# Two-layer hybrid backbone on one core: the order of the token blocks after the attention of the first layer

## The chip, the core and the metric

The kernel runs on one core of a Trainium2 chip, with its own engines: TensorE (PE: matmuls and transposes; PEld is its weight load), VectorE (DVE), ScalarE (ACT), GpSimd (POOL), and SyncE (SP), which issues the transfers. The metric is the device time of one execution in microseconds (us); less is better. A difference of 0.2% is 6.3 us.

## The reference

Two layers act on 1024 latent tokens and 256 context tokens, 1024 features each, in float32:

```python
def hybrid_layer(x, xc, c_act, cctx_act, ...):
    sh1, sc1, g1, sh2, sc2, g2 = split(c_act @ w_mod + b_mod, 6)     # and the same for the context
    u  = modulate(rmsnorm(x, n1), sh1, sc1) @ w_in                   # uc from xc
    ym = mlstm(u...); yn = neighbourhood_attention(u...); yl = rg_lru(u...)
    x = x + g1 * (concat([ym, yn, yl]) @ w_out)
    x = x + g2 * (square(relu(modulate(rmsnorm(x, n2), sh2, sc2) @ w1)) @ w2)
    # the context too, in the first layer alone
```

The modulation vectors of a layer (`c_act @ w_mod`, 6144 columns) depend on the conditioning only, so those of layer 1 can be computed anywhere in layer 0.

## The kernel before, in words

The residual stream is kept feature-major: 1024 features are 8 tiles of 128 partitions (K tiles), tokens lie along the free axis. The tokens form three blocks: block 0 is the context (256), blocks 1 and 2 are the halves of the latents (512 each). A matmul of 128x512 or 128x256 thus handles one K tile, one tile of 128 output columns and one block. Every float32 operand is split into a high and a low part (`xh`, `xlo`; `wh`, `wl`), and three matmuls make one product. ScalarE rounds the high part (L200 for weights, L210 for activations), VectorE subtracts for the low one (L201, L211).

The stages of a layer are the input projections with the mLSTM and the RG-LRU, the neighbourhood attention, the output projection, norm2 and the MLP. In the first layer:

- Attention. Half 0 of the output projection (the four K tiles that do not need the attention) is run between attention steps by `fill()`. A step of the attention ends with the transposes L688 and the products L714 and L718.
- Half 1 of the output projection. `y_load` (L1306) loads rows of the mixers' output `yT_d` into `yl` and splits them, K tile by K tile and, in a K tile, for blocks 0, 1, 2. The last K tile comes from the attention output `yr`. The buffer `yl` has three copies. `x_rows` (L1420) loads the residual `res`, L1325 are the matmuls, L1426 adds to the residual.
- `stat_add` (L373, L376, L377) squares each finished K tile on ScalarE and sums on GpSimd in `acc`; `stat_of` turns these sums over the partitions with TensorE (L383) and reduces them on VectorE (L385).
- `norm_block` takes the reciprocal root with small VectorE instructions (root steps, L167 to L180), spreads it with TensorE (L398), and then makes one K tile after the other: product (L410), `xh` (L411, ScalarE), `xlo` (L412).
- MLP. Eight groups of 512 hidden columns; each has four `w_mlp1` weights (projections L436) and four `w_mlp2` weights (matmuls L1477, added to the residual by L1481).

The work goes by `parts`, the sets of blocks that share a pass over the weights: `parts = [[0, 1], [2]]` (L1292) in layer 0, [[1], [2]] in layer 1. The first part goes through half 1 and norm2, then the second part through half 1; the first part goes through all MLP groups with the second's norm2 in group 0 (`ng`); then the second part's MLP, in the first groups of which the next layer's norm1 of the first part's blocks runs. The norm1 of the second part's blocks comes after the last group.

The modulation of layer 1 is 48 steps of `mod_step_e`: each loads 0.5 MB of `w_mod` (`mr`, L301) into a single buffer and makes, for two vectors, a product (L310) and seven products with sums (L312) on VectorE. `tick()` issues the next step; an MLP group calls it 8 times. Every two steps, TensorE transposes the products (L323) for the sum.

Program order is only a starting point: a scheduler orders the instructions of each engine ahead of time, and each engine then runs its queue in order; a waiting instruction holds back all that is behind it on its engine. Transfers issued by SyncE pass one hardware queue (q1). `issue_after` adds an edge to that order. PSUM banks are named by pools ("a", "b", "c", "p", "q"; tiles psa, psb, ...).

Of the kernel before, what the change touches and what calls it, by code (L numbers as in the profile page):

```python
# [21 lines left out]
P = 128  # L22
# [11 lines left out]
# column offsets inside the combined input projection  # L34
# [4 lines left out]
# token blocks: (offset, size, is_context)  # L39
# [3 lines left out]
def host_consts():  # L43
    """Arrays that depend on shapes alone."""
# [19 lines left out]
    # column mask: partitions (h, ic'), [3 column types, 32 key columns]  # L64
# [8 lines left out]
    # row mask: partitions (i', ic'), [group slot (1, 0), 12 key rows]  # L73
# [18 lines left out]
def backbone_kernel(ctx: ExitStack, tc: tile.TileContext, I, out, dbg=None):  # L92
# [9 lines left out]
    # the normalised blocks lie on one side, all else on the other; they change sides after each attention  # L102
# [23 lines left out]
    def bank(tag):  # L126
        """A PSUM bank; several tags take turns."""
# [37 lines left out]
    def rsqrt(x, tmp_i, tmp_z, y):  # L165
        """y = 1/sqrt(x) for positive x, to float32 accuracy (integer seed and Newton steps)."""
# [7 lines left out]
    def rsqrt_mean(ss, n, inv, tag):  # L174
        """1/sqrt(ss * inv + EPS) of a [P, n] tile of sums."""
# [10 lines left out]
    def load_w(src, shape, early=False):  # L186
        """Loads a float32 weight tile and splits it exactly into two float32r parts; early: in two steps, so that
        the first products start sooner."""
# [16 lines left out]
    def w_fm(w, l, c0, r0=0, kt=KT, cols=P):  # L205
        """Weight tile [P, kt, cols] of rows r0.. and columns c0.. of layer l."""
        return load_w(w[l, r0:r0 + kt * P, c0:c0 + cols].rearrange("(k p) c -> p k c", p=P), (kt, cols))
# [40 lines left out]
    # c_act, cctx_act: 32 columns per k tile (two used)  # L248
# [12 lines left out]
    def mod_step(l, j, rawpool, bufs, ptag, i=None):  # L261
        """128 modulation columns of both vectors; every fourth step finishes 512: of step j and the three before,
        or, when i says the place, of two steps each of shift and scale."""
# [32 lines left out]
    lastpe = [None]  # L296

    def mod_step_e(l, j, rawpool, bufs):
        """128 modulation columns without the column tiles: products and K tiles summed elementwise."""
        raw = rawpool.tile([P, KT, P], F32, name=nm("mr"), tag="mr", bufs=bufs)  # L300
        d = sp.dma_start(raw, I["w_mod"][l, :, j * P:(j + 1) * P].rearrange("(k p) c -> p k c", p=P))  # L301
        # the context needs only the first two vectors of the last layer
# [15 lines left out]
    def mod_sum(l, j, ns):  # L318
        """Sums over the partitions of the products of ns steps."""
# [262 lines left out]
    for l in range(DEPTH):  # L582
# [827 lines left out]
        with tc.tile_pool(name=f"mlp_{l}", bufs=1, reuse_waits="tile") as rp:  # L1410
# [109 lines left out]
            if not last:  # L1520
                run(next_norm(2))
# [35 lines left out]
```

## Time and profile before

| what | us |
|---|---|
| three runs | 3122.56, 3128.67, 3129.33 |
| median of the runs | 3128.67 |
| profiled execution, its span | 3122.6 |
| TensorE busy in the span | 3016.5 |

The profiled span equals the lowest of the runs to the last digit shown, so the execution has nothing measurable around its span. The busy time of TensorE can hide a low clock: the windows give the granted clock beside it, 1.00 being the full one. A wait is shown at the instruction that waits; its releaser is the instruction that came last.

### The profile page before, as it was taken

How to read it: one execution, taken by the hardware profiler on the slowest of the kernel's cores; microseconds unless marked ns; L12 is line 12 of the kernel's file. 1: busy time of each engine (PE TensorE's matmuls, PEld its weight loads, DVE VectorE, ACT ScalarE, POOL GpSimd, SP SyncE). 2: the span in 40 equal slices, each digit the busy share in tenths (PEclk: the TensorE clock that was granted, in tenths of full speed). 3: DMA queues.
4: the chain of work that ended last, by engine and by line, in shares of the span. 5: the costliest groups of instructions: out<-in, count | busy, mean ns of one | idle time of the engine just before them, and what ended most of it. 6: DMA issues, size and time to landing. Idle time of an engine off the chain costs nothing.

```text
span 3122.6 us, 47473 instructions
## 1 busy us (share of the span) xinstructions
PE 3016.5 (97%) x18250; PEld 2553.0 (82%) x18250; DVE 1898.7 (61%) x4318; ACT 1129.1 (36%) x2011; POOL 288.9 (9%) x252
## 2 busy tenths in 40 slices
PE   7999998999899999999999999998899999999999
PEld 6888887878788888887778889997787777887877
DVE  5757654887887666455444584755787444444444
ACT  4632223674422222233222453234564223332222
POOL 0410010122200000010000511002222000000000
PEclk9999999999899999999999999999999999999999
DMA  9624667865233444233333532348753332343333
GB/s 272 223 73 124 174 172 206 234 186 176 67 109 109 123 127 124 79 108 99 92 94 95 176 122 82 101 123 222 223 169 113 95 95 88 99 117 90 93 96 93
DMA packets 531098, 410.73 MB, mean 132 GB/s; under 512 B 27580, under 2 KB 496536, under 8 KB 530872
## 3 DMA queue, kind: packets, MB, share of 16 engines
q1 hardware_dynamic: 519448, 387.41, 42.1%
q0 software_dynamic: 8576, 15.00, 1.5%
q10 hardware_dynamic: 2848, 5.28, 0.6%
q8 instruction: 144, 2.36, 0.3%
q14 instruction: 82, 0.67, 0.1%
HBM read 339.72 MB, written 67.53 MB: 130 GB/s over the span
## 4 chain that ended last, share of the span: by engine, by line
PE 70%; DVE 11%; DMA 10%; issue 2%; ACT 2%; SPq 1%; POOL 0%; ACTq 0%; DVEq 0%; POOLq 0%
PE psa L436 15%; PE psa L1477 14%; PE psq L436 5%; PE psp L436 5%; PE psp L1477 5%; PE psq L1477 5%; PE psp L451 4%; DMA mr<-in_w_mod_dram 4%; PE psq L451 4%; PE psp L1325 2%; DVE ma L312 2%; PE psc L718 2%; DVE wl L201 1%; PE psa L1325 1%; PE psb L688 1%
## 5 line engine op out<-in xcount | busy, mean ns | idle before, releaser
L200 ACT ACTIVATE wh<-wr 128x1024 fp32r<-128x1024 f32 (+3 forms) x356 | 361.6, 1021 | 946.5 <-PE psa L1477 307.3
L201 DVE TENSOR_TENSOR wl<-wr,wh 128x1024 fp32r<-128x1024 f32 (+3 forms) x356 | 425.0, 1198 | 386.4 <-ACT wh L200 380.0
L436 PE MATMUL psa<-xlo,wh 128*128 128x512 f32 (+1 forms) x856 | 319.7, 374 | 2.2 <-DVE xlo L412 2.2
L436 PE MATMUL psa<-xh,wh 128*128 128x512 f32 (+1 forms) x856 | 319.4, 373 | 2.4 <-ACT xh L411 2.3
L436 PE MATMUL psa<-xh,wl 128*128 128x512 f32 (+1 forms) x856 | 319.6, 373 | 1.4 <-DVE wl L201 1.4
L1477 PE MATMUL psa<-hl,wh 128*128 128x512 f32 (+1 forms) x768 | 286.0, 373 | 0.6 <-DVE hl L211 0.6
L1477 PE MATMUL psa<-hh,wh 128*128 128x512 f32 (+1 forms) x768 | 284.2, 375 | 0.3 <-ACT wh L200 0.3
L1477 PE MATMUL psa<-hh,wl 128*128 128x512 f32 (+1 forms) x768 | 277.9, 373 | 0.6 <-DVE wl L201 0.6
L1481 DVE SCALAR_TENSOR_TENSOR res<-psa,modt,res 128x512 f32<-128x512 f32 (+1 forms) x192 | 131.0, 693 | 170.3 <-PE psa L1477 169.9
L436 PEld LDWEIGHTS psa<-xh,wh 128*128 128x128 f32 x856 | 162.1, 190 | 33.4 <-ACT xh L411 3.1
L436 PEld LDWEIGHTS psa<-xlo,wh 128*128 128x128 f32 x856 | 162.1, 189 | 33.1 <-DVE xlo L412 2.6
L436 PEld LDWEIGHTS psa<-xh,wl 128*128 128x128 f32 x856 | 162.1, 189 | 32.3 <-DVE wl L201 2.2
L377 POOL TENSOR_TENSOR acc<-acc,nsq 128x512 f32<-128x512 f32 (+1 forms) x56 | 77.9, 1401 | 1026.9 <-ACT nsq L376 976.5
L1477 PEld LDWEIGHTS psa<-hh,wh 128*128 128x128 f32 x768 | 144.3, 188 | 34.6 <-ACT wh L200 8.6
L451 PE MATMUL psp<-wl,xh 128*128 128x256 f32 (+1 forms) x560 | 164.0, 293 | 4.3 <-DVE wl L201 4.2
L1477 PEld LDWEIGHTS psa<-hh,wl 128*128 128x128 f32 x768 | 144.3, 188 | 28.7 <-DVE wl L201 1.5
L1477 PEld LDWEIGHTS psa<-hl,wh 128*128 128x128 f32 x768 | 144.4, 188 | 27.4 <-DVE hl L211 0.8
L210 ACT ACTIVATE hh<-rl 128x512 fp32r<-128x512 f32 (+1 forms) x160 | 93.5, 589 | 202.1 <-DVE rl L1453 202.0
L451 PE MATMUL psp<-wh,xh 128*128 128x256 f32 (+1 forms) x560 | 161.9, 289 | 2.4 <-ACT wh L200 2.4
L451 PE MATMUL psq<-wh,xh 128*128 128x256 f32 (+1 forms) x560 | 161.7, 289 | 1.4 <-ACT usq L605 0.9
L451 PE MATMUL psq<-wl,xh 128*128 128x256 f32 (+1 forms) x560 | 160.6, 287 | 0.0
L451 PE MATMUL psp<-wh,xlo 128*128 128x256 f32 (+1 forms) x560 | 159.9, 286 | 0.0
(409 smaller groups left out, 7328.5 us busy)
## 6 DMA issues: line engine op xcount, KB each, us to landing
wr<-in_w_mlp_dram SPq DMA_DIRECT2D x256, 512.0 KB
mr<-in_w_mod_dram SPq DMA_DIRECT2D x92, 512.0 KB
wr<-in_w_in_dram SPq DMA_DIRECT2D x48, 512.0 KB
tab<-T_d SPq DMA_DIRECT2D x48, 384.0 KB
T_d<-E_d POOLq DMA_DIRECT2D x48, 256.0 KB, 6.6
ab<-row_d SPq DMA_DIRECT2D x36, 256.0 KB
xT_d<-res SPq DMA_DIRECT2D x4, 2048.0 KB
wr<-in_w_out_dram SPq DMA_DIRECT2D x32, 256.0 KB
```

Of the source, the lines that this page charges most:

```text
L200: act.activation(hi[:, a:b], raw[:, a:b], AF.Copy)
L201: dve.tensor_sub(lo[:, a:b], raw[:, a:b], hi[:, a:b].bitcast(F32))
L210: act.activation(hi, src32, AF.Copy)
L312: dve.scalar_tensor_tensor(a, raw[:, k], s[:, k], a, op0=OP.mult, op1=OP.add)
L377: pool.tensor_add(acc[bi], acc[bi], sq[:, :n])
L436: m = pe.matmul(t[:, :n], w[a][:, k, :], X[bi][b][:, k, :], start=(i == 0), stop=(i == 23))
L451: pe.matmul(t[:, :cols], X[bi][b][:, half * 4 + k, o:o + P], ws[half][a][:, k, :], start=(i == 0), stop=(i == 23))
L688: pe.transpose(t[:w, j * P:(j + 1) * P], S[e][:, o:o + w], permT)
L718: pe.matmul(to[64 * e:64 * e + 64, :P], vals[i][:w, 64 * e:64 * e + 64], PT[:w, e, i], start=(i == 0), stop=(i == nt - 1))
L1325: pe.matmul(t[:, :n], w[a][:, k, cc * P:(cc + 1) * P], Y[bi][b][:, k], start=(i == 0), stop=(i == 11))
L1477: m = pe.matmul(t[:, :n], w[a][:, k, cc * P:(cc + 1) * P], H[bi, k][b], start=(i == 0), stop=(i == 3 * GH - 1))
L1481: dve.scalar_tensor_tensor(xr[bi][:, ct], t[:, :n], G2[:, ct, v:v + 1], xr[bi][:, ct], op0=OP.mult, op1=OP.add)
```

## The change

There are five edits. (1) In layer 0 the parts become [[2], [0, 1]]: block 2 goes first through the fill, half 1, norm2 and the MLP, then blocks 0 and 1 together. `norms2` runs the norm2 of blocks 0 and 1 one after the other within the first part's MLP groups. The norm1 of layer 1 runs within the second part's MLP for block 2, and after it for blocks 0 and 1; the LRU projections of layer 1 begin with block 2 (XR and GT are the recurrence's input and gate columns). `y_load` keeps its order over the blocks. (2) Where a norm has `acc` (both norm2 and norm1 of layer 1), the root steps hold their operands `x` and `z` in the PSUM bank `rb` into which the root is spread later. (3) `tick()` stands after the `w_mlp1` weights alone, so four a group. (4) The remaining steps come at the end of the second part (`tick(64)`). (5) The VectorE instructions of the first modulation step are ordered behind the last `xlo` of block 2's norm2 (`lastlo`, `held`). The rest of the change removes comments.

```diff
     def norm_block(l, which, bi, xt, ss, tp, res, acc=None):
...
-        rs = rsqrt_mean(ss, nt, 1.0 / D, f"nr{nt}")
         rb = bank("b")
+        if acc:
+            ti = sm.tile([P, nt], I32, name=nm("ri"), tag=f"nr{nt}i")
+            rs = sm.tile([P, nt], F32, name=nm("ry"), tag=f"nr{nt}y")
+            x, z = rb[:, 0:nt], rb[:, 8:8 + nt]
+            dve.tensor_scalar(x, ss, 1.0 / D, EPS, op0=OP.mult, op1=OP.add)
+            dve.tensor_scalar(ti, x.bitcast(I32), 1, None, op0=OP.arith_shift_right)
+            dve.tensor_scalar(rs.bitcast(I32), ti, -1.0, float(0x5F3759DF), op0=OP.mult, op1=OP.add)
+            for _ in range(3):
+                dve.scalar_tensor_tensor(z, rs, -0.5, x, op0=OP.mult, op1=OP.mult)
+                dve.tensor_mul(z, z, rs)
+                dve.scalar_tensor_tensor(rs, z, 1.5, rs, op0=OP.add, op1=OP.mult)
+        else:
+            rs = rsqrt_mean(ss, nt, 1.0 / D, f"nr{nt}")
...
-            dve.scalar_tensor_tensor(lo[:, k], t, SH[:, k, v:v + 1], hi[:, k].bitcast(F32),
-                                     op0=OP.add, op1=OP.subtract)
+            d = dve.scalar_tensor_tensor(lo[:, k], t, SH[:, k, v:v + 1], hi[:, k].bitcast(F32),
+                                         op0=OP.add, op1=OP.subtract)
+            lastlo[0] = d.ins
...
-                    proj_fm(w_fm(win, l, C_GT + ct * P), X, QB[:-1], evg[ct], banks="pqaaa")
+                    proj_fm(w_fm(win, l, C_GT + ct * P), X, [2], evg[ct], banks="pqaaa")
...
-                for bs in ([0, 1], [2]):
+                for bs in ([[2], [0, 1]] if l else [[0, 1], [2]]):
...
-                    proj_fm(w_fm(win, l, C_GT + ct * P), X, [2], evg[ct], banks="pqaaa")
+                    proj_fm(w_fm(win, l, C_GT + ct * P), X, QB[:-1] if l else [2], evg[ct], banks="pqaaa")
...
-        parts = [[1], [2]] if last else [[0, 1], [2]]
+        parts = [[1], [2]] if last else [[2], [0, 1]]
...
-                    tick()
+                    with (tc.issue_after(held) if held and i == 0 else nullcontext()):
+                        tick()
...
                 for c2 in range(KT // 2):
-                    tick()
...
+            def norms2(blks):
+                for bi in blks:
+                    yield from norm_block(l, 1, bi, xr[bi], stat_of(acc2, bi), yk, X2, acc2)
+
             for g in range(NG):
                 if g == 0:
-                    ng = norm_block(l, 1, 2, xr[2], stat_of(acc2, 2), yk, X2, acc2)
+                    afternorm = lastlo[0]
+                    ng = norms2(parts[1])
                     next(ng)
-                mlp_group(parts[0], g, ng)
-            tick(64)
+                mlp_group(parts[0], g, ng, afternorm if g == 0 else None)
...
-                if not last and g in (0, 1):
-                    ng = next_norm(g)
+                if not last and g < len(parts[0]):
+                    ng = next_norm(parts[0][g])
                     next(ng)
                 mlp_group(parts[1], g, ng)
+            tick(64)
             if not last:
-                run(next_norm(2))
+                for bi in parts[1]:
+                    run(next_norm(bi))
```

The changed kernel's lines are 14 to 16 higher around the output projection: L1341 is the matmul L1325, L1322 the load L1306, L1436 the load L1420, L729 and L733 the attention's L714 and L718.

The first place is SyncE's queue at the end of the first layer's attention, with the loads for half 1 of the output projection (`yl`) and of the residual (`res_9070` is block 0, `res_9071` block 1, `res_9072` block 2); `yl_9055` is the last load, the third K tile of block 2. Before:

```order
L1420 DMA res_9070<-xT_d 128x2x256
L1306 DMA yl_9051<-yT_d_86 128x512
L1420 DMA res_9071<-xT_d 128x2x512
L1306 DMA yl_9055<-yT_d_86 128x512
L1420 DMA res_9072<-xT_d 128x2x512 x4
L301 DMA mr_9748<-in_w_mod_dram 128x8x128
```

and now:

```order
L1436 DMA res_9071<-xT_d 128x2x512
L1322 DMA yl_9051<-yT_d_86 128x512
L1436 DMA res_9072<-xT_d 128x2x512 x4
L1322 DMA yl_9055<-yT_d_86 128x512
L302 DMA mr_9654<-in_w_mod_dram 128x8x128
L197 DMA wr_9292<-in_w_out_dram 128x4x256
```

The four loads of block 2's residual now stand ahead of `yl_9055`; before they stood behind it.

The second place is TensorE's queue where the attention ends. `xh_9017` is half 1's operand of block 0, `xh_9019` of block 1, `xh_9021` of block 2; the psc tiles are the attention's. Before, with the waits:

```order
L714 MATMUL psc_8819<-idj,rb_8817 128x128 [waits DVE_49]
L718 MATMUL psc_8819<-PT_8799,VB_8691 64x128 x6
L718 MATMUL psc_8819<-PT_8799,VC_8290 64x128 x4
L1325 MATMUL psa_9081<-xh_9017,wh_9074 128x256 [waits Activation_49]
L1325 MATMUL psp_9112<-xh_9017,wh_9074 128x256
L1325 MATMUL psa_9154<-xh_9017,wh_9147 128x256
L1325 MATMUL psa_9081<-xlo_9018,wh_9074 128x256 [waits DVE_49]
L1325 MATMUL psa_9081<-xh_9017,wl_9075 128x256
```

and now:

```order
L729 MATMUL psc_8991<-idj,rb_8989 128x128 [waits DVE_49]
L733 MATMUL psc_8991<-PT_8971,VB_8846 64x128 x6
L733 MATMUL psc_8991<-PT_8971,VC_8304 64x128 x4
L1341 MATMUL psa_9080<-xh_9021,wh_9074 128x512 [waits Activation_49]
L1341 MATMUL psa_9096<-xh_9021,wh_9074 128x512
L1341 MATMUL psp_9120<-xh_9021,wh_9114 128x512
L1341 MATMUL psq_9137<-xh_9021,wh_9114 128x512
L1341 MATMUL psa_9080<-xlo_9022,wh_9074 128x512 [waits DVE_49]
L1341 MATMUL psa_9080<-xh_9021,wl_9075 128x512
L1341 MATMUL psa_9080<-xh_9021,wh_9074 128x512 [waits Activation_49]
```

The matmuls of the output projection that stood between the last steps of the attention are gone from there; they begin behind the last step, with block 2, whose operands come from ScalarE.

The third place is VectorE's queue at the boundary of the layers, behind the last add to the residual (`L1481`). Before, where the norm of block 2 follows:

```order
L1481 SCALAR_TENSOR_TENSOR res_9072<-psa_17184,modt_119,res_9072 128x512
L201 TENSOR_TENSOR wl_17332<-wr_17330,wh_17331 128x1024
L201 TENSOR_TENSOR wl_17369<-wr_17367,wh_17368 128x1024
L385 TENSOR_REDUCE st_17207<-psc_17202 128x4
L180 TENSOR_SCALAR rx_17209<-st_17207 128x4
L167 TENSOR_SCALAR ri_17210<-rx_17209 128x4
L168 TENSOR_SCALAR ry_17212<-ri_17210 128x4
```

and now, where those of blocks 0 and 1 follow (`xlo_17162` is an operand of block 0, `st_17197` the sum of block 1, and `psb_17199` the bank of its root steps):

```order
L424 SCALAR_TENSOR_TENSOR psb_17184<-res_9070,scl_12600,psb_17144 128x256
L424 SCALAR_TENSOR_TENSOR acc_12461<-res_9070,scl_12600,psb_17144 128x256
L402 TENSOR_SCALAR psb_17199<-st_17197 128x4
L426 SCALAR_TENSOR_TENSOR xlo_17162<-psb_17184,modt_120,xh_17161 128x256
L403 TENSOR_SCALAR ri_17200<-psb_17199 128x4
L426 SCALAR_TENSOR_TENSOR xlo_17162<-acc_12461,modt_120,xh_17161 128x256
L404 TENSOR_SCALAR ry_17201<-ri_17200 128x4
L406 SCALAR_TENSOR_TENSOR psb_17199<-ry_17201,psb_17199 128x4
L407 TENSOR_TENSOR psb_17199<-psb_17199,ry_17201 128x4
L408 SCALAR_TENSOR_TENSOR ry_17201<-psb_17199,ry_17201 128x4
```

Two norms stand there in place of one: the root steps of block 1 come among the last K tiles of block 0, and its own eight K tiles behind them.

## Rows read from the trace of the kernel before

**Rows 1.** The page: span, and busy time by engine.
```profile
span 3122.6 us, 47473 instructions
...
PE 3016.5 (97%) x18250; PEld 2553.0 (82%) x18250; DVE 1898.7 (61%) x4318; ACT 1129.1 (36%) x2011; POOL 288.9 (9%) x252
```

**Rows 2.** Windows in norm2 of layer 0: length, busy us by engine, granted clock, DMA share, GB/s.
```profile
780.00:792.00 12.00, 8.12 (x25) 6.22 (x24) 10.03 (x24) 4.57 (x7) 8.19 (x4) 0.72 0.30 91
808.00:824.00 16.00, 11.38 (x56) 10.06 (x55) 14.62 (x32) 7.25 (x14) 2.59 (x2) 0.68 0.23 65
832.00:840.00 8.00, 7.26 (x45) 5.85 (x44) 6.05 (x9) 5.40 (x10) 0.00 (x0) 1.00 0.25 73
...
784.00:788.00 4.00, 2.34 (x7) 1.96 (x8) 2.61 (x6) 0.83 (x2) 2.84 (x2) 0.59 0.84 256
788.00:792.00 4.00, 4.00 (x12) 3.15 (x11) 3.41 (x6) 1.69 (x2) 1.74 (x1) 0.56 0.04 12
```

**Rows 3.** TensorE's waits, 740 to 860 us: total us, times, longest.
```profile
PE psc L383 <- POOL acc L377: 3.9, 1, 3.9
```

**Rows 4.** VectorE groups by shape: busy, mean ns, idle before.
```profile
L201 DVE TENSOR_TENSOR wl<-wr,wh 128x1024 fp32r<-128x1024 f32 x322 | 398.9, 1240 | 365.0 <-ACT wh L200 358.7
...
L1245 DVE COPY dn<-psb 128x4 f32<-128x4 f32 x36 | 5.5, 156 | 7.8 <-PE psb L1239 7.5
...
L170 DVE TENSOR_TENSOR rz<-ry 128x4 f32<-128x4 f32 x24 | 3.8, 159 | 0.5
```

**Rows 5.** Chain that ended last, end of the attention: start, us, what.
```profile
741.17 0.44 PE psq L688 x4
...
742.84 1.24 PE psc L718 x20
...
747.84 1.25 PE psc L718 x20
...
753.13 1.27 PE psc L718 x20
```

**Rows 6.** Timeline of SyncE at the end of the attention: start, us, instruction.
```profile
739.45 3.58 SPq L1420 DMA_DIRECT2D res<-xT_d  x7
743.48 0.33 SPq L1306 DMA_DIRECT2D yl<-yT_d  x1
743.86 0.46 SPq L1420 DMA_DIRECT2D res<-xT_d  x1
753.44 0.33 SPq L1306 DMA_DIRECT2D yl<-yT_d  x1
754.42 1.90 SPq L1420 DMA_DIRECT2D res<-xT_d  x4
```

**Rows 7.** Timeline of ScalarE, a split: in brackets the idle before, its releaser.
```profile
752.05 0.63 ACT L210 ACTIVATE xh<-yl 128x512 fp32r<-128x512 f32 x1 [1.65 <-DMA yl<-yT_d]
```

**Rows 8.** Windows at the end of the attention.
```profile
740.00:748.00 8.00, 8.00 (x71) 6.99 (x72) 2.90 (x7) 1.46 (x4) 0.00 (x0) 1.00 1.03 363
...
750.00:752.00 2.00, 2.00 (x16) 1.87 (x16) 0.69 (x1) 0.40 (x1) 0.00 (x0) 1.00 0.57 208
```

**Rows 9.** Chain at the boundary of the layers.
```profile
1732.54 5.59 PE psp L436 x24
```

**Rows 10.** VectorE's timeline there: two products of K tiles.
```profile
1747.23 0.75 DVE L410 SCALAR_TENSOR_TENSOR psb<-res,scl,psb 128x512 f32<-128x512 f32 x1 [0.93 <-PE psb L398]
...
1750.10 0.75 DVE L410 SCALAR_TENSOR_TENSOR psb<-res,scl,psb 128x512 f32<-128x512 f32 x1
```

**Rows 11.** A window in layer 1.
```profile
1866.00:1870.00 4.00, 1.61 (x13) 1.61 (x14) 2.94 (x3) 0.01 (x1) 1.25 (x1) 1.00 0.20 62
```

**Rows 12.** VectorE's waits over the span.
```profile
DVE ma L310 <- DMA mr<-in_w_mod_dram: 75.0, 36, 4.7
```

**Rows 13.** VectorE's timeline: nine products of modulation.
```profile
780.37 2.44 DVE L312 SCALAR_TENSOR_TENSOR ma<-mr,cact,ma 128x128 f32<-128x128 f32 x9
```

**Rows 14.** Window of the layer-1 modulation.
```profile
940.00:1060.00 120.00, 115.67 (x662) 98.93 (x661) 85.79 (x224) 26.18 (x41) 0.00 (x0) 1.00 0.39 112
```

More of the change, by code (lines that the diff above doesn't have):

```diff
@@ L296, in backbone_kernel @@
     lastpe = [None]
+    lastlo = [None]
     def mod_step_e(l, j, rawpool, bufs):
@@ L1443, in backbone_kernel, with mlp_group @@
             acc = {}
-            def mlp_group(part, g, ng=None):
+            def mlp_group(part, g, ng=None, held=None):
                 phase(f"mlp{l}")
```

## The prediction

> **What bounds the kernel.** I read the page first: TensorE is busy 3016.5 of 3122.6 us [rows 1], so a change pays where TensorE idles or runs at the low clock, and costs where it takes such a cover away. I then cut the span into windows, to find such places near the code that is changed. There is one, norm2 of layer 0 [rows 2]. From 780 to 792 us TensorE is busy 8.12 of 12 us at a mean granted clock of 0.72, from 808 to 824 us 11.38 of 16 at 0.68, from 832 to 840 us 7.26 of 8. The reader is to see there that busy time alone hides half of the loss: TensorE is busy 4.00 of 4.00 us from 788 to 792, at a clock of 0.56. TensorE's waits name the start of the hole: the transposes L383 of a block's sums wait 3.9 us for GpSimd's adds L377 [rows 3]. VectorE is nearly full in these windows (10.03 of 12, 14.62 of 16). It makes the norms of blocks 0 and 1 while only block 2's matmuls, with no norm in them, are there to cover. Last I read the two stretches that the change puts in another order, the end of the attention [rows 5 to 8] and the boundary of the layers [rows 9, 10], and what surrounds the layer-1 modulation [rows 12 to 14].
>
> **Term 1, the norm2 hole goes: -15.2 us.** Full-speed work lost in a window is its length less busy time times clock: 12 - 8.12 x 0.72 = 6.2, 16 - 11.38 x 0.68 = 8.3, and 8 - 7.26 = 0.7, in sum 15.2 [rows 2]. Now the norm of block 2 alone stands between its half of the output projection and the MLP. Its cover is the projection of blocks 0 and 1: 8 column tiles of 12 matmuls at 0.233 and 12 at 0.117 us (24 matmuls of 512 columns take 5.59 us [rows 9]), 33.6 us. Under it lie 12 root steps at 0.2 us (an instruction of 0.159 [rows 4] and its gap) and eight K tiles at 1.43 us (two in 1750.10 - 1747.23 = 2.87 [rows 10]), 13.8 us. The modulation's products, which fill VectorE in that stretch, are held behind it. Norm2 of blocks 0 and 1 then has the first two MLP groups as cover. If the cover fails, half of the hole comes back (the rival "still a hole").
>
> **Term 2, the end of the attention: +10.2 us.** Between 737.9 and 759.2 us TensorE is always busy, with little attention in it: three steps of products of 1.24 to 1.27 us, each with a broadcast of 0.2 ahead, and ten transposes, 0.44 us for four [rows 5], make 5.5 us. The other 15.8 us are matmuls of half 1, of blocks 0 and 1, which lie between the steps. In the new order they aren't there: the last attention steps stand bare, and half 1 starts with block 2. Of it only two K tiles for four banks can run, 2 x 4 x 3 = 24 matmuls, 5.6 us [rows 9]; the next waits for the split of the last load, `yl_9055`. When does that land? In the trace the ring is full from 740 to 748 us at 363 GB/s, and drains at about 751.1 (208 GB/s in the window from 750 to 752, 208 / 363 of its 2 us) [rows 8]. A load issued at 743.48 us, behind the residual's [rows 6], releases ScalarE only at 752.05 [rows 7], so loads land in the order of issue, some 0.95 us after the drain. Now the four loads of block 2's residual (four of 128 x 2 x 512 x 4 bytes, 2.1 MB) stand ahead of `yl_9055` (0.26 MB), where they stood behind it. At 0.363 MB/us that is 6.5 us: 751.1 + 6.5 + 0.95 + 0.63 for the split gives 759.2. By then 5.6 us of half 1 is done in place of 15.8, so 10.2 us are lost. The bound below: `yl_9055` comes when it is wanted, and only the bare steps remain. I put the attention's end between 744.5 and 746.5 then; with the later one 8.6 us hold 5.5 us of work, a loss of 3.1. The bound above: the four residual loads start late, as the attention's buffers come free (they wait for TensorE), which delays `yl_9055` by up to 3 us more, 13.2. I take 10.2, since the order of the queue forces it.
>
> **Term 3, the clock after that gap: +2.7 us.** In the trace the clock falls to 0.59 and 0.56 of the full one, about 1.2 of 2.4 GHz, behind the gap at 780 us, which costs 2.34 x 0.41 + 4.00 x 0.44 = 2.7 us [rows 2]. The gap of term 2 is longer. Bounds 0 and 4.
>
> **Term 4, the boundary of the layers: +4.3 us.** Before, one norm remains behind the MLP, block 2's, while blocks 0 and 1 are ready to be projected. TensorE passes from the MLP to the next projection at T = 1732.54 without a gap [rows 9], and the products of the norm run from 1747.23 on [rows 10]. Now block 2 is ready, and the norms of 0 and 1 follow. The cover is GT and XR of block 2 (4 x 24 matmuls, 22.4 us) and XR of block 0 (5.6 us). In TensorE's new queue the broadcast of block 1's root stands at T + 26.4, behind most of XR of block 0. Its K tiles need 8 x 1.43 = 11.4 us, so the last comes at T + 37.8. The first column tile of XR of block 1 goes at that pace: 22 matmuls, 5.1 us of work, in some 9 us. Behind it 74 matmuls are left to the end of the gate projection, 17.3 us: T + 55.1. All the matmuls to that point (worth 216 of 512 columns, 50.4 us, and 0.6 us of transposes) take 51.0 us without a stall; the loss is some 4.3. Bounds: 0, if the scheduler's neighbours fill in, and 6. The clock here I leave at full: TensorE was busy 1.61 of 4 us from 1866 to 1870 at a clock of 1.00 [rows 11], a lower share than the 5.1 of 9 here.
>
> The Trainium skill, "TensorE: Matmul & The Clock Gate", section "HAM oscillation — how this bites in real kernels", says against this that a TensorE which goes idle for operands between groups of matmuls falls back to the low clock and pays the rise each time. The trace agrees behind the gap at 780 us (0.59) and not from 1866 to 1870 us (1.00) [rows 2, 11]. By the rule the boundary would cost another 2.7 us, and the sum would be +4.7; by the second row term 3 would go too, and it would be -0.7.
>
> **Term 5, the modulation: 0 us.** A step is 16 products at about 0.27 us (nine in 2.44 [rows 13]), 4.3 us of VectorE. Before, 8 steps lie in a group of blocks 0 and 1 (67.2 us of TensorE), 0.51 us of VectorE for one of TensorE. Now it is 4 in a group of block 2 (44.8 us), 0.39. Against that the eight weight splits at 1.24 us [rows 4] come every 44.8 us, not 67.2 (0.22 against 0.15), and the norm2 of two blocks (6.4 + 11.4 + 4.8 for the roots, 22.6 us) lies in two such groups, 0.25 against 13.8 / 67.2 = 0.21. The sum is about the same load. Before, it costs TensorE 120 - 115.67 = 4.3 us between 940 and 1060 us [rows 14]. I let that stand. Bounds: -4.3, if the slower pace frees TensorE of it, and +16.7, if VectorE becomes the bound (below).
>
> **Term 6, root steps in PSUM: 0 us.** 12 instructions a norm. One on SBUF operands takes 159 ns, a copy out of PSUM 156 ns [rows 4]; the norms are covered, or counted above. If they were 0.1 us slower each, the boundary would lose 2 x 12 x 0.1 = 2.4 us, and as much the other way.
>
> **Sum.** -15.2 + 10.2 + 2.7 + 4.3 = +2.0 us on the profiled execution, 3124.6. Its span of 3122.6 equals the lowest of the three runs, so nothing is to be added around it, and the median lies 6.1 us above. Against the median of 3128.67 the forecast is **3130.7 us**: no change that a measurement of this kernel can tell, for which 0.2%, 6.3 us, is needed.
>
> **Rivals.**
> - *The loads come in time.* For it: `yl_9055` is small, and if the residual's loads of blocks 0 and 1 start earlier than before the ring is empty sooner. Against it: the order of the queue. Term 2 is then 3.1 and term 3 is 0: -15.2 + 3.1 + 4.3 = -7.8, 3120.9; with the boundary covered as well -12.1, 3116.6. Chance 0.30, of it 0.27 measurably faster.
> - *VectorE becomes the bound (the other side).* Place: the first two MLP groups of block 2. VectorE runs in order, and a product that waits for its weights holds back the splits of hidden tiles that TensorE needs next. It waited 75.0 us in 36 waits, 2.1 each [rows 12]; 8 steps with 2.1 us, 16.7 us, on a VectorE that is full. It decides once its work and waits in a group pass the group's 44.8 us of matmuls. For it: one weight buffer. Against it: before, the waits lay in spare time, and the cost to TensorE was 4.3 us in all. +18.7, 3147.4. Chance 0.13.
> - *The boundary is covered.* Term 4 is 0, as when the norm of block 1 gets ahead of XR of block 0: -2.3, 3126.4. For it: TensorE is never idle there now; against it: the order. Chance 0.13, of it 0.02 faster.
> - *Still a hole.* The change doesn't do what it says: block 2's sums, too, end late on GpSimd, since VectorE's weight splits still slow it, and half of term 1 returns, 7.6: +9.6, 3138.3. Chance 0.06.
> - *The forecast*: 0.38, with a range of its own from 3123 to 3139; of it 0.24 within 0.2% and 0.14 above.
>
> Together: faster 0.27 + 0.02 = 0.29, within 0.2% 0.24 + 0.03 + 0.11 = 0.38, slower 0.14 + 0.13 + 0.06 = 0.33. The range, 3115 to 3147, reaches from the first rival's low end to the edge of the second.
>
> **What would show it.** Term 1: no window of 4 us between the end of the attention and the MLP below 3.9 us of TensorE, save the gap of term 2, and no wait of L383 for GpSimd. Terms 2 and 3: TensorE waits some 6 us or more for ScalarE's `xh` behind the attention, ScalarE for the DMA of `yl`, and the clock is near 0.5 behind it. Term 4: waits of L436 for `xlo` in some 9 us about 29 us behind the last MLP matmul of layer 0, at full clock. Term 5: TensorE's waits for L1453 or L211 in the first groups stay under 2 us. I am wrong if the gap behind the attention is under 5 us, or if the MLP of block 2 shows TensorE idle by more than 5 us.

## The result, and the profile after

The changed kernel takes 3160.93 us in the median (3156.28 to 3164.15), the kernel before, on the same chip, 3129.0 us: a ratio of 1.0098, 95% interval 1.0079 to 1.0117. It is slower by some 32 us, outside the range that was given. The page's first part, of the changed kernel, answers to [rows 1]:

```profile
span 3154.5 us, 47460 instructions
...
PE 3029.3 (96%) x18250; PEld 2557.5 (81%) x18250; DVE 1899.4 (60%) x4318; ACT 1128.8 (36%) x2011; POOL 287.3 (9%) x252
```

The span is 31.9 us longer, and the share of TensorE is lower. Every run for which a span is on record takes 1.7 to 1.9 us more than its span (3156.28 and 3154.5 us here). The equality of span and lowest run before, from which the prediction took that nothing lies around the span, was then most likely one of two different executions; nothing below rests on it. A profile shows one execution, whose time is not the median: here it is the lowest of four, in experiments 2 and 4 the highest of four, 12 to 13 us above the median, and in experiment 8 the highest of nine.

To find the stages, I took windows of 10 us over both traces and summed 10 less busy time times granted clock, which is TensorE's lost work at full speed. Worked out from these windows, the changed kernel's loss less that of before is:

| stage of the trace | lost more, us | foretold, us |
|---|---|---|
| 0 to 720 us, through the attention | +8.8 | 0 |
| 720 to 780 us, end of the attention | +12.6 | +12.9 (terms 2 and 3) |
| 780 to 840 us, norm2 | -15.4 | -15.2 (term 1) |
| 840 to 1260 us, MLP of block 2 | +17.2 | 0 (term 5) |
| 1260 to 1740 us, MLP of blocks 0 and 1 | -0.6 | 0 |
| 1740 to 1800 us, boundary of the layers | +3.1 (another 0.4 to 1810 us) | +4.3 (term 4) |
| 1800 to 3110 us, layer 1 | +4.2 | 0 |

The borders of the stages lie some microseconds apart in the two traces, so a row is good to a few. The windows of the changed kernel, with the columns of [rows 2], show the norm2 hole gone, and TensorE idle in the MLP that follows (it lost 4.3 us in that place before [rows 14], and now 4.0, 2.4 and 6.3 us by idle time alone, which is 12.7 of the 21.5 us that it loses there; the other 8.8 us go to windows at a low clock):

```profile
780.00:840.00 60.00, 60.00 (x314) 50.55 (x313) 47.29 (x100) 26.50 (x40) 24.61 (x19) 1.00 0.29 88
840.00:960.00 120.00, 116.02 (x494) 90.60 (x493) 104.01 (x249) 41.27 (x57) 0.00 (x0) 0.97 0.41 123
960.00:1080.00 120.00, 117.62 (x508) 92.71 (x507) 91.34 (x207) 31.63 (x39) 0.00 (x0) 1.00 0.46 137
1080.00:1240.00 160.00, 153.67 (x673) 121.91 (x672) 103.97 (x203) 47.28 (x65) 11.59 (x7) 0.96 0.46 138
```

**The MLP of block 2.** TensorE's waits from 835 to 1240 us (in total, times, longest) are for VectorE above all (0.9 us, once, is for ScalarE's split L200); the largest:

```profile
PE psa L1494 <- DVE wl L201: 4.8, 5, 1.3
PE psa L1494 <- DVE res L1498: 2.4, 5, 1.0
```

and VectorE's own waits there are for the modulation's weights, and for TensorE's transposes of the products, which free their buffers:

```profile
DVE ma L311 <- DMA mr<-in_w_mod_dram: 42.5, 27, 4.1
...
DVE ma L311 <- PE psc L324: 10.9, 3, 3.6
```

TensorE's stalls come about once in a group, and they are of two kinds. Until 930 us, in the first two groups, it loses 7.1 us. There VectorE is nearly full, with the K tiles of norm2 of two blocks beside the products of the modulation; the one wait for a weight in this window takes 0.69 us:

```profile
900.00:920.00 20.00, 17.48 (x62) 12.41 (x61) 19.22 (x37) 7.59 (x10) 0.00 (x0) 0.83 0.28 80
```

From 930 us on it loses 14.4 us, and VectorE has time to spare. Here four waits of 3.8 to 4.1 us for a modulation weight each stand directly ahead of a stall, and these four stalls make 13.8 of the 14.4 us. VectorE's timeline shows one (start, us, instruction, in brackets the idle before and its releaser):

```profile
1099.74 0.29 DVE L311 TENSOR_SCALAR ma<-mr,cact 128x128 f32<-128x128 f32 x1 [4.11 <-DMA mr<-in_w_mod_dram]
1099.94 0.74 DVE L1498 SCALAR_TENSOR_TENSOR res<-psq,modt,res 128x512 f32<-128x512 f32 x1
1100.61 0.34 DVE L313 SCALAR_TENSOR_TENSOR ma<-mr,cact,ma 128x128 f32<-128x128 f32 x1
1100.87 1.40 DVE L1498 SCALAR_TENSOR_TENSOR res<-psa,modt,res 128x512 f32<-128x512 f32 x2
...
1103.11 2.35 DVE L201 TENSOR_TENSOR wl<-wr,wh 128x1024 fp32r<-128x1024 f32 x2
```

The product L311 waits for `mr`, and behind it wait the adds L1498, which empty PSUM banks, and the next weight splits L201. TensorE's timeline has the other end of it:

```profile
1100.74 0.50 PE L1494 MATMUL psq<-hh,wh 128*128 128x512 f32 x1 [1.24 <-DVE res L1498]
...
1101.76 0.76 PE L1494 MATMUL psa<-hh,wh 128*128 128x512 f32 x1 [0.29 <-DVE res L1498]
...
1104.38 0.80 PE L1494 MATMUL psp<-hh,wl 128*128 128x512 f32 x1 [0.58 <-DVE wl L201]
```

It waits for banks (L1498) and then for the split (L201), and the clock falls, to 0.66 from 1100 to 1110 us. VectorE is busy 4.12 of the 10 us before, and 7.79 of these 10:

```profile
1090.00:1100.00 10.00, 9.45 (x40) 7.04 (x38) 4.12 (x12) 2.64 (x3) 0.00 (x0) 1.00 0.40 123
1100.00:1110.00 10.00, 8.39 (x22) 5.96 (x23) 7.79 (x15) 0.00 (x0) 0.00 (x0) 0.66 0.37 105
```

Over the whole stretch VectorE's work is that of before (third busy time: 296.79 us before, then 299.31 us now):

```profile
840.00:1240.00 400.00, 395.67 (x2271) 342.73 (x2270) 296.79 (x732) 94.94 (x143) 0.00 (x0) 1.00 0.40 117
840.00:1240.00 400.00, 387.31 (x1671) 305.21 (x1670) 299.31 (x657) 120.18 (x161) 11.59 (x7) 0.97 0.45 133
```

**The end of the attention.** SyncE's timeline has the loads in the order that was read off, `yl_9055` last, behind four loads of the residual:

```profile
749.30 3.80 SPq L1436 DMA_DIRECT2D res<-xT_d  x6
755.34 0.33 SPq L1322 DMA_DIRECT2D yl<-yT_d  x1
757.19 1.90 SPq L1436 DMA_DIRECT2D res<-xT_d  x4
759.75 0.33 SPq L1322 DMA_DIRECT2D yl<-yT_d  x1
```

ScalarE splits it 9 us later, after 5.5 us without work:

```profile
768.62 0.63 ACT L210 ACTIVATE xh<-yl 128x512 fp32r<-128x512 f32 x1 [5.50 <-DMA yl<-yT_d]
```

and TensorE runs 24 matmuls, at a granted clock of 0.62 from 756 to 760 us and 0.52 from 760 to 764, and then waits again:

```profile
756.54 0.62 PE L733 MATMUL psc<-PT,VC 128*64 128x128 f32 x8
758.05 1.22 PE L1341 MATMUL psa<-xh,wh 128*128 128x512 f32 x2 [0.89 <-ACT xh L210]
...
769.30 0.73 PE L1341 MATMUL psa<-xh,wh 128*128 128x512 f32 x2 [2.78 <-ACT xh L210]
```

The attention itself ends at 757.2 us, not between 744.5 and 746.5: the trace is some 9 us late there already, and its last steps, with nothing between them, wait 1.11 us for ScalarE's `PT` and 0.99 and 2.33 us for VectorE's `yr`:

```profile
755.57 0.33 PE L729 MATMUL psc<-idj,rb 128*128 128x128 f32 x1 [2.33 <-DVE yr L842]
```

**The boundary.** The broadcast of block 1's root lets the first product start at 1782.59 us, two K tiles take 2.87 us, as in [rows 10],

```profile
1782.59 0.76 DVE L424 SCALAR_TENSOR_TENSOR psb<-res,scl,psb 128x512 f32<-128x512 f32 x1 [3.50 <-PE psb L412]
...
1785.46 0.75 DVE L424 SCALAR_TENSOR_TENSOR psb<-res,scl,psb 128x512 f32<-128x512 f32 x1
```

and TensorE is busy 2.79 to 3.08 of 4 us while they last, at a clock of 1.00 throughout:

```profile
1784.00:1788.00 4.00, 2.79 (x11) 1.48 (x10) 3.79 (x6) 2.13 (x4) 0.00 (x0) 1.00 0.00 0
1788.00:1792.00 4.00, 3.07 (x11) 1.55 (x10) 3.90 (x7) 1.42 (x3) 0.00 (x0) 1.00 0.00 0
1792.00:1796.00 4.00, 3.08 (x13) 2.25 (x13) 2.04 (x9) 2.85 (x6) 1.55 (x4) 1.00 0.02 4
```

### The profile page after: what moved, and what is told of

The parts are those of the page before. It is cut to its first block, busy times and chain, and to the rows that moved or that the text cites. A ratio compares the mean times of both kernels' runs of the same rounds, so it can differ in the third digit from the quotient of the medians.

```text
span 3154.5 us, 47460 instructions
## 1 busy us (share of the span) xinstructions
PE 3029.3 (96%) x18250; PEld 2557.5 (81%) x18250; DVE 1899.4 (60%) x4318; ACT 1128.8 (36%) x2011; POOL 287.3 (9%) x252
## 5 line engine op out<-in xcount | busy, mean ns | idle before, releaser
L200 ACT ACTIVATE wh<-wr 128x1024 fp32r<-128x1024 f32 (+3 forms) x356 | 361.5, 1021 | 965.0 <-PE psa L1494 298.4
L201 DVE TENSOR_TENSOR wl<-wr,wh 128x1024 fp32r<-128x1024 f32 (+3 forms) x356 | 425.6, 1200 | 373.5 <-ACT wh L200 366.5
L1498 DVE SCALAR_TENSOR_TENSOR res<-psa,modt,res 128x512 f32<-128x512 f32 (+1 forms) x190 | 129.9, 694 | 173.9 <-PE psa L1494 173.3
L451 PEld LDWEIGHTS psa<-xh,wh 128*128 128x128 f32 x872 | 164.0, 188 | 31.7 <-ACT wh L200 0.9
L210 ACT ACTIVATE hh<-rl 128x512 fp32r<-128x512 f32 (+1 forms) x160 | 93.7, 589 | 189.1 <-DVE rl L1469 189.1
```

Source lines behind the costliest of these rows:

```text
L200: act.activation(hi[:, a:b], raw[:, a:b], AF.Copy)
L201: dve.tensor_sub(lo[:, a:b], raw[:, a:b], hi[:, a:b].bitcast(F32))
L210: act.activation(hi, src32, AF.Copy)
L451: m = pe.matmul(t[:, :n], w[a][:, k, :], X[bi][b][:, k, :], start=(i == 0), stop=(i == 23))
L1498: dve.scalar_tensor_tensor(xr[bi][:, ct], t[:, :n], G2[:, ct, v:v + 1], xr[bi][:, ct], op0=OP.mult, op1=OP.add)
```

## The experiments

The theory after these traces: the loss in the MLP of block 2 comes from the modulation's steps in VectorE's queue, each of which can hold the queue for its weights, under a cover of 5.6 us a weight; the loss behind the attention from the order of the loads. The rivals stand in each expectation. All medians are of runs beside the kernel before on the same chip (3128.25 to 3131.41 us), so ratios are compared. The stage sums of an experiment are those of its one profiled execution.

**1. Modulation in the second part alone.**

```diff
-                    with (tc.issue_after(held) if held and i == 0 else nullcontext()):
+                    if part is parts[1]:
                         tick()
...
                 for c2 in range(KT // 2):
+                    if part is parts[1] and c2 % 2 == 0:
+                        tick()
...
-                if not last and g < len(parts[0]):
-                    ng = next_norm(parts[0][g])
+                if not last and g == 4:
+                    mod_scale(1, 0)
+                    ng = next_norm(2)
```

> The changed kernel with the 48 modulation steps of layer 1 moved out of block 2's MLP groups into those of blocks 0 and 1 (six a group; norm1 of block 2 then in group 4). Theory: VectorE, held up by the modulation's products and their weights, is what stalls TensorE in block 2's MLP (about 17 us from 840 to 1260 us): 3161 - 17, some 3144 us, with TensorE idle under 3 us in that MLP. Rival: the splits of the weights, at one in 5.6 us, and two norms fill VectorE by themselves: no more than 5 us are won, 3156 or above.

Measured: 3137.51 us, ratio 1.0028 (1.0016 to 1.004), 23 us under the changed kernel. The window of the MLP of block 2:

```profile
840.00:1240.00 400.00, 399.49 (x1793) 322.50 (x1792) 210.39 (x311) 124.93 (x166) 10.59 (x7) 1.00 0.32 97
```

TensorE is idle for 0.5 of 400 us, so the weight splits and two norms by themselves don't hold it. The stage loses 3.8 us less than before did, 21 us less than the changed kernel. The rival is out. The steps that were moved cost nothing in their new place, though VectorE waits 26.7 us in 23 waits for their weights there (1240 to 1740 us):

```profile
1260.00:1740.00 480.00, 480.00 (x2754) 417.45 (x2753) 335.37 (x767) 125.97 (x194) 16.22 (x14) 1.00 0.38 114
```

The edit also drops the hold. Nothing then keeps the first modulation steps behind norm2, and the scheduler put two of the 48 there, from 769 us on; the other 46 run where the text says. By its text the changed kernel has 32 of the 48 steps in block 2's MLP, and the rest already behind it; these 32 are what the edit moves.

**2. Block 2's loads first.**

```diff
-        y_load(Y, QB, 1, yk)
-        for bi in QB:
-            off, n, isc = BLKS[bi]
-            split(Y[bi][0][:, 3], Y[bi][1][:, 3], yr[:, off:off + n])
+        for part in parts:
+            y_load(Y, part, 1, yk)
+            for bi in part:
+                off, n, isc = BLKS[bi]
+                split(Y[bi][0][:, 3], Y[bi][1][:, 3], yr[:, off:off + n])
```

> The changed kernel with half 1's loads of block 2 traced, and queued, ahead of those of blocks 0 and 1. Theory: the order of the loads opens the hole behind the attention, so the stall for xh (2.8 us), and with it most of the wait for the third K tile, goes: 3 to 6 us, 3155 to 3158 us. Rival: the bytes in the ring bound it, whatever their order, since the residual is wanted at the same time; or the bare attention steps are most of the loss: within 2 us of 3161.

Measured: 3153.62 us, ratio 1.008 (1.0055 to 1.0106), 7.3 us under the changed kernel; the intervals of the two overlap, and the trace is the clearer sign. In SyncE's timeline the twelve residual loads and the six of blocks 0 and 1 now follow:

```profile
750.00 11.08 SPq L1437 DMA_DIRECT2D res<-xT_d  x12
761.50 2.43 SPq L1322 DMA_DIRECT2D yl<-yT_d  x3
```

and TensorE's gap behind the attention is 0.9 us:

```profile
750.00:760.00 10.00, 7.42 (x79) 5.90 (x80) 4.30 (x12) 4.83 (x13) 0.00 (x0) 1.00 0.91 304
760.00:770.00 10.00, 10.00 (x44) 8.08 (x43) 3.88 (x6) 1.60 (x3) 0.00 (x0) 1.00 1.05 365
```

The stage from 720 to 780 us loses 2.9 us more than before, in place of 12.6. What is left are the bare steps (waits of 0.6 to 0.7 us, three times) and that gap, at full clock. The order of the loads it was; the ring's bytes alone don't make the hole.

**3. The fill in the order of before.**

```diff
-                for part in parts:
+                for part in (parts if last else [[0, 1], [2]]):
                     phase(f"oproj{l}")
                     Yh = ...
```

> The changed kernel with the half of the output projection that fills the attention in the order of before, blocks 0 and 1 first. Theory: the 7 us that are lost from 540 to 720 us, beside the attention, come from the fill's order: 3154 us. Rival: they come from the scheduling of the attention itself, or are made up later: 3159 to 3163.

Measured: 3160.24 us, ratio 1.0097 (1.0081 to 1.0113): nothing. In its trace the stages through 720 us lose 2.7 us more than before, in place of 8.8, but the MLP of block 2 loses 21 us. At 720 us the profiles of kernels whose text is the same up to there differ, too: 5.6 us in experiment 1, 13.0 in experiment 2, 8.1 in experiment 5. One profiled execution alone can't tell 7 us in the attention. All profiles together can: from 540 to 720 us TensorE loses 11.2 to 13.0 us in the four kernels with the order of before (before, and experiments 7, 9 and 10) and 19.0 to 24.1 us in the seven that fill block 2 first; experiment 3 lies between, at 15.8. So a loss of 6 us and more beside the attention does belong to the changed order. Part of it lies from 580 to 600 us, where the new fill has passed from block 2 to block 0 and waits 2.0 us for that block's split `yh` (L210). There the seven lose 3.0 to 6.8 us, and the five kernels with the old fill nothing (below: before, experiment 3, the changed kernel):

```profile
580.00:600.00 20.00, 20.00 (x191) 17.95 (x190) 16.56 (x52) 12.17 (x34) 7.26 (x4) 1.00 0.66 193
580.00:600.00 20.00, 20.00 (x184) 18.00 (x184) 16.41 (x52) 11.98 (x34) 7.29 (x4) 1.00 0.70 199
580.00:600.00 20.00, 17.16 (x133) 14.28 (x128) 14.78 (x52) 11.29 (x33) 7.21 (x4) 0.91 0.65 186
```

The median of experiment 3 doesn't show that the old fill wins this back, and what makes the rest of the loss stays open.

**4. The order of the parts alone.** The kernel before with `parts = [[2], [0, 1]]` and what follows from it, but a tick at every weight and no hold:

```diff
-                    with (tc.issue_after(held) if held and i == 0 else nullcontext()):
-                        tick()
+                    tick()
...
                 for c2 in range(KT // 2):
+                    tick()
```

with `tick(64)` behind the first part and the roots in SBUF (the diff is against the changed kernel).

> The kernel before with the order of the parts changed alone: eight modulation steps a group, none held, root steps in SBUF. Theory (VectorE is the bound in block 2's MLP): 8 x 4.3 = 34 us of products beside 10 us of weight splits and 16 us of the rest do not go into 44.8 us, so six groups lose 10 us and more each: 3180 to 3210 us. Rival: the pace of four a group or the holding back is what costs: below 3155.

Measured: 3151.77 us, ratio 1.0078 (1.0055 to 1.0102). The theory's 3180 to 3210 us fails. The time is where the rival put it, below 3155, but not for the rival's reason: the MLP of block 2 loses 17.0 us more than before, as in the changed kernel, with neither the pace of four nor the hold. VectorE's waits there:

```profile
DVE ma L311 <- DMA mr<-in_w_mod_dram: 51.2, 31, 4.5
```

The kernel asks for eight steps a group, but it didn't run them at that pace: 37 loads are issued up to 1240 us, against 34 in the changed kernel, in nearly the same time:

```profile
L302 SPq DMA_DIRECT2D mr<-in_w_mod_dram x37: 367/368/1227, 770.3 to 1231.2; - x37
...
L302 SPq DMA_DIRECT2D mr<-in_w_mod_dram x34: 367/368/458, 760.4 to 1231.2; - x34
```

So the run tells nothing of a doubled pace. It shows that four ticks a group in place of eight, and the hold, bought nothing in this MLP, and that about the same steps under block 2's weights cost the same again. The working of 10 us a group had another fault as well: a step makes 16 products only in the first 16 of the 48 steps, which serve two vectors; the other 32 make 8. The median is 9 us under the changed kernel's, with intervals that overlap; I don't know from which edit.

**5 and 6. Experiments 1 and 2 together, with the roots in PSUM and in SBUF.**

> The edits of the first two experiments together on the changed kernel: modulation in the second part's MLP, and block 2's loads of half 1 first. Theory: they take away two separate losses, 23.4 and 7.3 us, so the time is some 3130 us, level with before. Rival: the second only moves the wait, or the first already took part of it: 3135 or above.

> The kernel of the experiment above with the root steps in SBUF again. Theory: they are on no path that sets the end, but at the boundary, where the two norms stand; no difference that can be measured, 0 to 3 us. In the first parts-only kernel that boundary lost 0.7 us, with the roots in PSUM 3 to 4 us; rival: the roots in PSUM cost those 3 us, which the window from 1740 to 1800 us shows.

Measured: 3129.26 us, ratio 1.0003 (0.9989 to 1.0016), and 3128.03 us, ratio 0.9993 (0.998 to 1.0006). The two losses add, 23.4 + 7.3 of the 31.9 us (by the ratios 0.70% and 0.18%, of 0.95% that go with both), and with both gone the changed order stands level with before. Level isn't free of losses: experiment 5's trace still loses 9.1 us more than before from 540 to 720 us, 2.9 at the end of the attention and 4.2 at the boundary, and pays for them with what it wins in norm2, 10.1 us, and in the MLP of block 2, 3.8. In norm2 the changed kernel won 15.4. Both experiments drop the hold, as experiment 1 does, and the first two modulation steps run among norm2 again, from 769 to 803 us, so the changed order may have a little more to give; that was not tried.

The roots make no difference that the medians can tell. In the traces they cost a little at the boundary: from 1740 to 1810 us the six profiles of the changed order with roots in PSUM lose 3.4 to 4.2 us, the two with roots in SBUF, experiments 4 and 6, 2.0 and 2.2. (The 0.7 us of experiment 4 in the expectation stop at 1800 us, where its boundary is not over.)

**7. The kernel before with the hold alone.**

```diff
-                    tick()
+                    with (tc.issue_after(held) if held and i == 0 else nullcontext()):
+                        tick()
...
+                    afternorm = lastlo[0]
                     ng = norm_block(l, 1, 2, xr[2], stat_of(acc2, 2), yk, X2, acc2)
```

> The kernel before, with its order of the parts, and the first modulation step held behind the last xlo of the first part's norm2 as the only edit. Theory: the products of the modulation on VectorE (from 765 to 785 us) make the norm2 hole; held back, about half of the 15 us goes: 3119 to 3123 us. Rival: two norms with only block 2's matmuls as cover make it, whatever else VectorE does: 3126 to 3131.

Measured: 3122.06 us, ratio 0.9976 (0.9965 to 0.9987): faster than both kernels, as expected. Its windows:

```profile
776.00:840.00 64.00, 60.81 (x296) 50.23 (x295) 54.03 (x119) 28.71 (x48) 15.29 (x12) 0.95 0.22 66
940.00:1060.00 120.00, 113.26 (x639) 97.52 (x640) 85.59 (x224) 26.39 (x42) 0.00 (x0) 0.99 0.39 112
```

TensorE is busy 60.81 of 64 us in norm2; the stage from 780 to 840 us loses 8.9 us less than before. Part is given back: from 940 to 1060 us it is idle for 6.7 us, where it was 4.3 [rows 14]. In both kernels these are above all waits of TensorE's modulation transposes L323 (here L324) for VectorE's products, 6.2 us in seven waits here and 3.5 in five before, and hardly any for splits or banks.

**8. The changed kernel with the modulation's weights in halves.** Two buffers of four K tiles take the place of one of eight, so that a load can run beside the products of the other half:

```diff
-        raw = rawpool.tile([P, KT, P], F32, name=nm("mr"), tag="mr", bufs=bufs)
...
+        for h in range(2):
+            raw = rawpool.tile([P, KH, P], F32, name=nm("mr"), tag=f"mr{h}", bufs=bufs)
...
+                for k in range(h * KH, (h + 1) * KH):
```

> The changed kernel with each modulation weight loaded as two halves in two buffers of half the size, so that a load can begin while the other half is being used; the products are the same, in another order. Theory: VectorE's waits for the single buffer (42.5 us in 27 waits in block 2's MLP) hold TensorE, and fall by half or more: 3161 - 8 to 12 us, 3149 to 3153. Rival: the products themselves, put in a burst ahead of the splits in VectorE's queue, hold it: 3157 or above.

Measured: 3145.61 us, ratio 1.0047 (1.0032 to 1.0061), 15 us under the changed kernel. VectorE's waits in block 2's MLP, and TensorE there:

```profile
DVE ma L316 <- DMA mr<-in_w_mod_dram: 21.7, 18, 2.1
DVE ma L316 <- PE psc L329: 21.2, 7, 3.6
```

```profile
840.00:1240.00 400.00, 391.10 (x1733) 311.36 (x1732) 308.18 (x683) 124.58 (x169) 10.97 (x7) 1.00 0.46 136
```

The waits for the weights fall from 42.5 to 21.7 us (another 2.5 stand at L318), the loss of the stage from 17.2 to 6.2 us. Up to 930 us the stage still loses 3.5 us (7.1 in the changed kernel), and after that 7.0 (14.4). The products are the same and VectorE is busy longer (308.18 us for 299.31), so it is the waiting for weights in VectorE's queue, more than the work, that holds TensorE. Not every wait counts alike: those for TensorE's transposes grow from 10.9 to 21.2 us, and the sum of both kinds falls only from 53.4 to 45.4.

**9 and 10. The hold and the half loads on the kernel before, with the roots in SBUF and in PSUM.**

> The kernel before with the modulation held behind norm2 and its weights loaded as two halves. Theory: the idle time of TensorE from 940 to 1060 us, 6.7 us with the hold, comes from the waits for the single weight buffer, and goes too: 3115 to 3118 us. Rival: with eight steps a group VectorE is full there whatever the buffers, so 3121 to 3124.

> The kernel of the experiment above with the root steps of the norms in PSUM, as in the change. Theory: GpSimd's adds make VectorE's root steps late only where both read SBUF (L172 took 297 ns in the mean before, 159 ns in the changed kernel), and norm2 of blocks 0 and 1 is on the path, so 1 to 3 us are won against the experiment above. Rival: nothing that can be measured, within 1 us.

Measured: 3120.76 us, ratio 0.9971 (0.9958 to 0.9983), and 3124.58 us, ratio 0.9986 (0.9974 to 0.9998). Neither can be told from experiment 7, so the theory of experiment 9, 3115 to 3118 us, fails. Where its trace is better,

```profile
940.00:1060.00 120.00, 116.63 (x663) 101.05 (x663) 91.94 (x246) 28.60 (x45) 0.00 (x0) 0.99 0.45 132
```

(3.4 us idle from 940 to 1060 us, not 6.7) it is by less than the runs scatter. In this kernel the half loads hardly shorten VectorE's waits for weights, 65.0 us in place of 69.3. The gain expected of PSUM roots in experiment 10 is not there.

## Why the prediction was wrong

- **Term 1** was right: -15.4 us by the windows for -15.2. Either part of the change takes much of the hole by itself: the new order without the hold 12.5 us (experiment 4), the hold without the new order 8.9 us in experiment 7 (11.6 and 4.9 in the profiles of 9 and 10, which hold as well).
- **Terms 2 and 3** were right in their sum, 12.6 for 12.9 us, and in the cause: experiment 2 moves the loads and 9.7 us go. That the sum fits so well is partly luck. The working has a wait of some 7 us for `xh`, and calls itself wrong with a gap under 5; the two waits make 3.7. Against that the attention's last steps waited 4.4 us among themselves, where the working has 3.1 for bare steps, and the low clock took 3.8 us for 2.7. The moment of the attention's end was missed by over 10 us.
- **Term 4** was right in mechanism: the pace of K tiles as read, and no fall of the clock. It measured 3.1 us to 1800 and 3.4 to 1810 us, for 4.3 (the working's own figures, 55.1 - 51.0, give 4.1); TensorE was busy for more of that time than the 5.1 of 9 us forecast. The section of the Trainium skill that the prediction set against this ("TensorE: Matmul & The Clock Gate", "HAM oscillation — how this bites in real kernels") has a case in which the wait for a load is longer than the matmuls between two such waits, and there the clock goes low each time. The trace agrees behind the attention, where matmuls of 1.6 us stood between waits of 0.99 and 2.33 us (0.62 and 0.52). The boundary is not that case: its pauses are of 0.6 us and less, and the clock stayed at 1.00 with TensorE busy 2.79 of 4 us.
- **Term 5 is the step that failed**: 0 us forecast, 17.2 measured. I compared VectorE's average load in a group, found about the same as before, and let the old 4.3 us stand. The load is indeed about the same, 296.79 us of 400 before and 299.31 now, and TensorE loses 4.3 us before and 21.5 now. (The 16 products of a step hold for the first 16 of the 48 steps only, the other 32 have 8. That lowers both sides of the comparison and doesn't save it.) What the working left out is where a wait stands: in VectorE's queue, ahead of adds and splits that TensorE needs soon. Experiment 1 takes the steps away and 21 us go; experiment 8 leaves the work, halves the waits for weights, and 11 us go. Before, VectorE waited 75.0 us in 36 waits [rows 12], more than the 42.5 us in 27 now, and TensorE hardly noticed: there a `w_mlp2` weight covers 24 matmuls of each of blocks 0 and 1, 2 x 12 x (0.233 + 0.117) = 8.4 us, so a wait of 2.1 us and a step's products fit in. Block 2 alone gives 5.6 us a weight. No run changed this cover alone, but experiment 1 comes near: six steps in 67.2 us are the pace of four in 44.8, and under the weights of blocks 0 and 1 they cost nothing. In the first two groups the K tiles of norm2 stand in the same queue and fill it, and a third of the loss, 7.1 us, lies there.
- That was in part the rival "VectorE becomes the bound", to which I gave 0.13. Its 16.7 us are close to the 17.2 by luck: it put them all into the first two groups, on a VectorE that is full, and two thirds came later, behind single long waits on a VectorE that is not. By its point of decision, work and waits beyond 44.8 us a group, it would have been dismissed there: from 940 to 1240 us VectorE's busy time and the waits of these products come to 38 us in 44.8.
- **Term 6** was right for the runs: none tells roots in PSUM from roots in SBUF. The traces put 1 to 2 us at the boundary on them, within the 2.4 us that the working allows.
- The measured terms, -15.4 + 12.6 + 3.1 + 17.2, make 17.5 us. Of the rest of the 31.9, 8.8 us come through the attention of layer 0, which the prediction put at nothing without a look at the fill: that some 6 us or more of it belong to the new order is shown by the twelve profiles together, its whole cause isn't. The 4.2 us of layer 1 are not settled: the order of before alone ranges over 7 us there. Experiments 1 and 2 together give 31.7 us back, but the swap's gain in norm2 is in that balance, so the medians don't show these two to be the only losses.

## What to carry to other kernels

When a change gives a matmul stage fewer columns per weight, ask what VectorE's queue holds there that can wait for a transfer: the cover per weight has to take one such wait and the work behind it, and the average load does not show this. A wait that costs nothing in one stage is paid for in another. Look up in the trace, too, where instructions ran whose edges were dropped or whose pace was changed: twice here a kernel did not run what its text seemed to ask for. When blocks change places, the loads of the block that goes first must change places with them. And a single edit of a change may hold the gain: here the order edge alone, on the old kernel, gave 0.24% where the whole change lost 1%.

## What the runs showed of the hardware

VectorE's small root step with both operands in SBUF took 297 ns in the mean before (L172, 128x4), most of them about 160 ns and some of them 1.25 us (at 798.60 us, while GpSimd was adding from 798.35 us for 1.48 us). With one operand in PSUM that step takes 159 ns in the mean of 18 (L408, changed kernel):

```profile
L172 DVE SCALAR_TENSOR_TENSOR ry<-rz,ry 128x4 f32<-128x4 f32 x24 | 7.1, 297 | 0.4
...
798.60 1.25 DVE L172 SCALAR_TENSOR_TENSOR ry<-rz,ry 128x4 f32<-128x4 f32 x1
...
798.35 1.48 POOL L377 TENSOR_TENSOR acc<-acc,nsq 128x512 f32<-128x512 f32 x1 [2.24 <-ACT nsq L376]
...
L408 DVE SCALAR_TENSOR_TENSOR ry<-psb,ry 128x4 f32<-128x4 f32 x18 | 2.9, 159 | 0.4
```

Six such steps that stay in SBUF in the changed kernel, in the first norm of layer 0, take 159 ns too, so two operands in SBUF alone don't make a step long. That GpSimd's adds are the cause of the long ones was not tried. Roots in PSUM won no time here.

The length of one pause does not tell what TensorE's clock does behind it. In the MLP of block 2 the clock fell to 0.66 behind a wait of 1.24 us at 1100 us, and stayed at 1.00 behind one of 1.32 us at 1055 us, though TensorE was busy 9.45 and 10.00 of the 10 us before these windows.

And one execution differs from another of the same text by some 7 us through the attention (5.6 to 13.0 us, experiments 1 and 2), so a stage there is to be compared over several profiles, and checked against medians.
